# A decoder layer on one core: one-hot operations on pairs of 16-bit values, gate steps spread equally, and some weight products in 512-column matmuls

## The chip, the core and the metric

The kernel runs on one core of a Trainium2 chip. The metric is the device time of one launch in microseconds, lower is better. The engines are TensorE (PE in the profile; PEld is its loading of weights), VectorE (DVE), ScalarE (ACT), GpSimd (POOL) and SyncE (SP), which issues most of the loads. They run side by side, each through its own list of instructions in order, and wait for each other by semaphores.

## The reference, cut to what matters

256 tokens and 16 meta tokens of width 2048 pass through one layer in fp32:

```
h    = layer_norm(concat(meta, x))
proj = h @ w_in          # pool 1024 | z 3072 | x 3072 | B 1024 | C 1024 | dt 48
mix  = concat(pool_mix(pool), ssd(x, B, C, dt) * silu(z), normed by group) @ w_out
h    = layer_norm(ALPHA * h + mix)
q    = h @ wq            # 8 heads x 2 x 128: scores against 128 keys each,
                         # top 16 of each side, top 16 of the 256 sums -> i1, i2, gate
act  = gelu(h . u[i1 * 128 + i2])                       # 8 x 16 of 16384 experts a token
out  = layer_norm(ALPHA * h + sum_k gate_k * act_k * v[i1 * 128 + i2])
```

## The kernel before

Every product with a weight is made from two parts. A value is split into a high part (float32r, a rounded copy) and a low part (the rest), and three of the four products are summed in PSUM: high weight x high input, high weight x low input, low weight x high input. Weights come in units of 128 x 1024 (eight blocks of 128 x 128) in the order of `W_ORDER`; `next_unit` (line 116) issues the load on SP's queue three units ahead, ScalarE copies the high part `wh` (line 129), VectorE subtracts for the low part `wl` (line 130), with three buffers of each. `mm_unit` (line 199) makes the 24 matmuls of a unit, eight for each of the three products, 256 to 272 columns each: `wh` with the high input, `wh` with the low input, `wl` with the high input. A block of 128 output columns takes two units (`kh` 0 and 1).

The stages follow each other: layer norm and transposition; the `w_in` stage (72 blocks; in each of eight groups two for B and C, three for x, three for z, with the SSD work of the group before as `side` steps between units, by `tick`); the `w_out` stage, whose matmuls have 512 columns of the weight as the moving operand; the second layer norm, into `h1H` and `h1L`; 16 blocks of `wq` with the routing as side steps; 128 blocks of `u` (`u_block`, line 612); and the `v` stage.

The kernel doesn't gather rows of `u`. It computes `h . u` for all 16384 experts, densely, with the experts on partitions, and multiplies by a dense gate. `gate_steps` (line 750) makes the gate for four tokens at a time, in 64 steps for each half of the experts (half 1 while blocks 0 to 63 of u run, half 0 while blocks 64 to 127 run). The routing leaves the indices `iT` and the gates `gT` (a high and a low part) transposed, with the 128 chosen slots of a token on partitions. A step makes three one-hot tiles in fp16: `o2` (VectorE, 4 x 128: iota equal to the second index), `oe` (VectorE, 4 x 64: iota equal to the first index), and `o1` (GpSimd, 4 x 2 x 64: `oe` times the two gate parts). Eight matmuls of 64 columns per step multiply `o2` by `o1`. Each of these tiles has two buffers, and the matmuls of a step are issued with the one-hots of the step after it. Every two steps the PSUM tile `pg` is full: for half 1 ScalarE writes it into the tile `a1` as the gate that u's activations will be multiplied with (line 622); for half 0 VectorE multiplies it into `a0`, which already holds the activations (line 784).

In blocks 0 to 63 the number of gate steps after block b is

```python
n = -(-left // max(62 - b, 1))
tick(n)
left -= n
```

from the block on in which the routing is through (`left` starts at 65: 64 steps and one that only issues the last matmuls). In blocks 64 to 127 it is one and two in turn.

When a half is complete, `flag_steps` and `slot_steps` find for each expert row whether a token of either half of the tokens chose it, and give it a slot (`pos`). `scatter` (line 723) writes the activation rows of one block to `acd` in DRAM, by an indirect DMA on POOL's queue: for half 1 as blocks 72 to 122 pass, straight from `pos`; for half 0 from the last u blocks on, from small copies (`paced`) that VectorE makes behind the product of a block. The `v` stage begins with two dense blocks (`a_dense`), then SP loads slots of rows (`ac`, line 998), POOL gathers the rows of `v` that belong to them (`rawv`, line 1003), and TensorE multiplies; `a_split` (line 1015) splits the activations into `v_scr`. `ac` lies in the memory of `a1`; `v_scr` and the residual `rr` lie in that of `h1L` and `h1H`.

The order of instructions on each engine is not that of the source alone: a scheduler of the framework orders them at build time by its own estimates of cost, except where `keep_in_program_order` or `issue_after` pins them. Dependences and buffer releases are tracked tile by tile.

Of the kernel before, what the change touches and what calls it, by code (L numbers as in the profile page):

```python
# [2 lines left out]

# [1 line left out]

# [18 lines left out]
NL1 = 3  # L24
NQ1 = 3
NLB = 4
NDB = 2


# [33 lines left out]
def tile_layer(ctx: ExitStack, tc: tile.TileContext, x, meta, pk, pk48, w_in, w_dt, w_pool,  # L63
# [129 lines left out]

    front = ExitStack()
    hTp = front.enter_context(tc.tile_pool(name="hTp", bufs=1))
    hTH = hTp.tile([P, KC, L], F32R, name="hTH")
    hTL = hTp.tile([P, KC, L], F32R, name="hTL")

    def mm_unit(ps, xh, xl, kh, m, n, t0=0):

# [270 lines left out]
    for g in range(NG):  # L471
        bT = conv(24 + g, 0, "bT", 2)
        cc = conv(32 + g, 12, "cc", 2)
        xT = [conv(3 * g + j, 0, "xT", 6) for j in range(3)]
        zs = []
        side.append(group_steps(g, bT, cc, xT, zs))
        for j in range(3):
            pz = proj(NMETA)
            z = sp.tile([P, T], F32, tag="zs", name="zs", bufs=4)
            act.activation(z, pz[:, :T], AF.Silu)  # L480
            zs.append(z)


# [65 lines left out]

    lws = ExitStack()  # L550
    h1ps = []

    def w_out_body1(i):
        if i == 0:
            h1ps.append(ctx.enter_context(tc.tile_pool(name="h1p", bufs=1, side="right", reuse_waits="tile")))
            h1ps.append(h1ps[0].tile([P, KC, T], F32R, tag="h1H", name="h1H"))
            h1ps.append(h1ps[0].tile([P, KC, T], F32R, tag="h1L", name="h1L"))
            lw = lws.enter_context(tc.tile_pool(name="lw", bufs=1, side="right", reuse_waits="tile"))
            hold(range(2 + 144 + 64 - NL1, 2 + 144 + 64), lw)

# [10 lines left out]
                dve.bn_stats(sts[tt][:, c], hs[tt][:, cs])  # L571
    lp = lnp[0]
    lws.close()
    h1p, h1H, h1L = h1ps
# [37 lines left out]
    def u_block(b):  # L612
        ps = ps_tile("psu")
        for kh in range(2):
            mm_unit(ps, h1H, h1L, kh, P, T)
        if b < 64:
            act.activation(a_half[0][:, b, :T], ps[:, :T], AF.Gelu)
        else:

            act.activation(ps[:, :T], ps[:, :T], AF.Gelu)  # L620
            g = a_half[1][:, b - 64, :T]
            i = dve.tensor_mul(g if b < P - NDB else a_dense[:, b - (P - NDB)], g, ps[:, :T])  # L622
            if pos[0] is not None and n_sc[0] < HALF[0][1]:

                tc.keep_in_program_order(i)
# [94 lines left out]
    paced = []  # L720
    behind = [None]

    def scatter(half, b):
        at = paced.pop() if paced and not half else pos[half][:, b:b + 1]
        with tc.issue_after(behind[0].ins):
            i = pool.indirect_dma_start(  # L726
                out=acd[half][:, :], out_offset=bass.IndirectOffsetOnAxis(ap=at, axis=0),
                in_=a_half[half][:, b, :], in_offset=None)

        i = getattr(i, "ins", i)  # L730
        if b:
            tc.declare_no_dep(i, group=f"rows{half}", reason="rows of their own")
        tc.add_to_no_dep_group(f"rows{half}", i)

    def scatter_0():
        if n_sc[0] < HALF[0][1]:
            scatter(0, n_sc[0])
            n_sc[0] += 1

    def zero_steps():  # L740
# [9 lines left out]
    def gate_steps(half):  # L750


        io = iota[:, half * 64:(half + 1) * 64]
        pg = None
        ohs = []
        t0 = 0
        while t0 < T or ohs:
            wait = half == 0 and ranked[1] is not None
            if t0 < T and not wait:
                o2 = ohp.tile([P, 4, P], F16, tag="o2", name="o2", bufs=2)  # L760
                oe = ohp.tile([P, 4, 64], F16, tag="oe", name="oe", bufs=2)
                o1 = ohp.tile([P, 4, 2, 64], F16, tag="o1", name="o1", bufs=2)
                i1, i2 = (it[:, t0:t0 + 4].unsqueeze(2) for it in iT)
# [94 lines left out]
    def softmax_steps():  # L858
        for tt in range(2):
# [12 lines left out]
                pe.transpose(ps[:, i * P:(i + 1) * P], s[:, tt], ident)  # L872
            ts = slice(tt * P, (tt + 1) * P)
            for i in range(2):
                dve.tensor_copy(iT[i][:, ts], ps[:, i * P:(i + 1) * P])
            gs = rp.tile([P, P], F32, tag="gs", name="gs")
            dve.tensor_scalar(gs, ps[:, 2 * P:3 * P], GSC, None, ALU.mult)
            dve.tensor_copy(gT[:, ts, 0], gs)
            dve.tensor_sub(gT[:, ts, 1], gs, gT[:, ts, 0])
            yield  # L880

    for j in range(16):
        if j < NQ1:
            ps = pre[j]
            tick()
        else:
            ps = ps_tile("psq1")
            mm_unit(ps, h1H, h1L, 0, P, T)
            tick()
        mm_unit(ps, h1H, h1L, 1, P, T)  # L890
        tick()
        act.copy(qT[:, j, :], ps[:, :T])
# [10 lines left out]
    a_dense = slp.tile([P, NDB, T], F32, name="a_dense")  # L903
# [4 lines left out]
    iT = [ohp.tile([P, T], F16, name=f"iT{i}", bufs=1) for i in range(2)]  # L908
    gT = ohp.tile([P, T, 2], F16, name="gT", bufs=1)
    def flag_tick(n):  # L910
        while n and flagq:
            if next(flagq[0], flagq) is flagq:
# [5 lines left out]
    for b in range(64):  # L918
        u_block(b)
        if a_half[1] is None:  # L920
            tick(RT_TICKS)
            if not side:
# [22 lines left out]

    for b in range(64, 128):
        u_block(b)
        if pos[1] is not None:
            due = min(b - 64, -(-(P - NDB - 64) * (b - 72) // 50), P - NDB - 64)
            while n_sc[1] < due:  # L950
                scatter(1, n_sc[1])
                n_sc[1] += 1
        if side:
            tick(2 if b % 2 else 1)
            flag_tick(1)
        else:
            if paced:
                scatter_0()
            rank_0()
    drain()  # L960
    while pos[0] is None:
        rank_0()
    while n_sc[1] < P - NDB - 64:
        scatter(1, n_sc[1])
        n_sc[1] += 1


    rrt = h1p.tile([P, 2, D], F32, tag="h1H", name="rr")
    rr = [rrt[:, tt] for tt in range(2)]
    v_scr = h1p.tile([P, 16, T], F32R, tag="h1L", name="v_scr")  # L970
    ap1s.close()
# [43 lines left out]
    def a_split(i):  # L1015
# [9 lines left out]
        src = a_dense[:, b - (P - NDB)] if what == "d" else acs[i]  # L1025
# [155 lines left out]
```

## Time and profile before

| | |
|---|---|
| median of 3 runs | 2069.78 us (2066.89 to 2072.77) |
| profiled execution | 2070.15 us, its span 2068.5 us |
| mean granted TensorE clock | 0.993 |
| PE busy | 2012.2 us (97%), 14780 matmuls |
| DVE busy | 1573.7 us (76%) |
| ACT busy | 1115.4 us (54%) |
| POOL busy | 519.6 us (25%) |
| stages in the span (from the timeline) | w_in to about 510 us, w_out to 690, wq to 797, u to 1584, v to the end |

The profile is one execution. A busy time is the union of an engine's instructions; matmuls overlap in it, so a matmul's own duration is not its price, and the distance between the starts of two is. Numbers at the end of tile names are left out, so `o1` and `o2` are both `o` in the rows (o2 is written at line 764, o1 at 768). A wait in brackets is the idle time of the engine before an instruction, with what ended it.

### The profile page before, as it was taken

The page shows a single profiled execution, that of the slowest core. Times are in us where ns is not written, and L with a number is a line of the kernel's source. Part 1 is how long each engine was busy: PE and PEld are TensorE (multiplying, and loading weights), DVE is VectorE, ACT ScalarE, POOL GpSimd, SP SyncE. Part 2 cuts the span into 40 slices and gives each one's busy share as a digit, 9 for nine tenths or more (in the row PEclk, how much of TensorE's full clock was granted, in tenths as well). Part 3 has the DMA queues.
Part 4 walks back from the last instruction along what each step waited for, and adds up shares of the span by engine and source line. Part 5 has one row for each costly group of instructions (what it writes and reads, how often), then busy time and mean ns, then how long its engine had stood idle before and what let it go on. Part 6 is the DMA issues. An engine that isn't in the chain of part 4 may idle for free. (4 is left out here: it accounts for less than half of the span.)

```text
span 2068.5 us, 37549 instructions
## 1 busy us (share of the span) xinstructions
PE 2012.2 (97%) x14780; PEld 1859.8 (90%) x14780; DVE 1573.7 (76%) x2542; ACT 1115.4 (54%) x1637; POOL 519.6 (25%) x423
## 2 busy tenths in 40 slices
PE   7999999999999899999899999999999999999997
PEld 6999999999878799999899999999998777878885
DVE  6767777777654878999899979999954555656667
ACT  6457777777433544445459573333343555555563
POOL 1000000000000000000455525566334674232231
PEclk9999999999999999999999999999999999999999
DMA  5555555554775465665445556666678999778884
GB/s 160 187 179 173 177 180 177 174 178 160 255 235 197 158 204 175 184 183 175 150 146 167 173 173 196 199 191 197 199 223 270 300 323 330 273 268 288 295 310 150
DMA packets 113970, 430.75 MB, mean 208 GB/s; under 512 B 14112, under 2 KB 27808, under 8 KB 98800
## 3 DMA queue, kind: packets, MB, share of 16 engines
q1 hardware_dynamic: 89168, 282.29, 44.5%
q0 software_dynamic: 24336, 145.53, 19.7%
q8 instruction: 116, 1.90, 0.4%
q10 hardware_dynamic: 288, 0.52, 0.1%
q14 instruction: 62, 0.51, 0.1%
HBM read 407.20 MB, written 21.09 MB: 207 GB/s over the span
## 5 line engine op out<-in xcount | busy, mean ns | idle before, releaser
L129 ACT CAST wh<-raw 128x1024 fp32r<-128x1024 f32 (+1 forms) x502 | 525.8, 1047 | 662.3 <-PE psu L204 352.2
L130 DVE TENSOR_TENSOR wl<-raw,wh 128x1024 fp32r<-128x1024 f32 (+1 forms) x502 | 629.9, 1256 | 277.8 <-ACT wh L129 264.0
L130 DVE TENSOR_TENSOR wl<-rawv,wh 128x1024 fp32r<-128x1024 f32 x210 | 256.8, 1224 | 171.0 <-ACT wh L129 160.1
L1040 PE MATMUL psv<-wh,v_scr 128*128 128x512 f32 x1304 | 363.2, 398 | 11.4 <-ACT v_scr L1027 6.3
L129 ACT CAST wh<-rawv 128x1024 fp32r<-128x1024 f32 x210 | 220.3, 1049 | 205.8 <-PE psv L1040 109.0
L768 POOL TENSOR_TENSOR o<-oe,gT 128x512 f16<-128x512 f16 x128 | 200.1, 1574 | 475.7 <-DVE oe L766 291.7
L1040 PEld LDWEIGHTS psv<-wh,v_scr 128*128 128x128 f32 x1304 | 245.8, 190 | 75.4 <-ACT v_scr L1027 8.8
L204 PE MATMUL psu<-h1H,wh 128*128 128x256 f32 x2048 | 292.6, 285 | 0.0
L204 PE MATMUL psu<-h1L,wh 128*128 128x256 f32 x2048 | 286.2, 282 | 0.0
L204 PE MATMUL psu<-h1H,wl 128*128 128x256 f32 x2048 | 284.3, 281 | 0.0
L204 PEld LDWEIGHTS psu<-h1H,wh 128*128 128x128 f32 x2048 | 261.5, 189 | 0.0
L204 PEld LDWEIGHTS psu<-h1L,wh 128*128 128x128 f32 x2048 | 261.2, 189 | 0.0
L204 PEld LDWEIGHTS psu<-h1H,wl 128*128 128x128 f32 x2048 | 260.9, 188 | 0.0
L1040 PE MATMUL psv<-wl,v_scr 128*128 128x512 f32 x652 | 206.2, 395 | 0.0
L1003 POOL DMA_INDIRECT rawv<-in_v,ac x105 | 123.6, 1177 | 236.2 <-DVE wl L130 195.8
L204 PE MATMUL psj<-hTH,wh 128*128 128x272 f32 (+5 forms) x1168 | 177.3, 294 | 1.3 <-ACT hTH L185 0.8
L204 PE MATMUL psj<-hTL,wh 128*128 128x272 f32 (+5 forms) x1168 | 166.1, 284 | 0.0
L204 PE MATMUL psj<-hTH,wl 128*128 128x272 f32 (+5 forms) x1168 | 165.9, 284 | 0.0
L726 POOL DMA_INDIRECT acd<-a,flags x114 | 136.6, 1199 | 94.1 <-DVE a L622 32.6
L204 PEld LDWEIGHTS psj<-hTH,wh 128*128 128x128 f32 (+1 forms) x1168 | 154.2, 189 | 5.0 <-ACT hTH L185 1.8
L204 PEld LDWEIGHTS psj<-hTL,wh 128*128 128x128 f32 (+1 forms) x1168 | 151.9, 187 | 0.2
L204 PEld LDWEIGHTS psj<-hTH,wl 128*128 128x128 f32 (+1 forms) x1168 | 151.6, 187 | 0.0
(252 smaller groups left out, 2234.1 us busy)
## 6 DMA issues: line engine op xcount, KB each, us to landing
raw<-in_u SPq DMA_DIRECT2D x256, 512.0 KB
raw<-in_w_in SPq DMA_DIRECT2D x144, 512.0 KB
raw<-in_w_out SPq DMA_DIRECT2D x64, 512.0 KB
raw<-in_wq SPq DMA_DIRECT2D x32, 512.0 KB
ac<-acd SPq DMA_DIRECT2D x105, 128.5 KB
clb<-cd POOLq DMA_DIRECT2D x8, 816.0 KB
x<-in_x SPq DMA_DIRECT2D x4, 512.0 KB
gb<-in_ln_nat POOLq DMA_DIRECT2D x2, 1024.0 KB
```

Of the source, the lines that this page charges most:

```text
L129: act.copy(wh[:, :n], raw[:, :n])
L130: dve.tensor_sub(wl[:, :n], raw[:, :n], wh[:, :n].bitcast(F32))
L204: pe.matmul(ps[:m, :n], w[:, k * m:(k + 1) * m], xx[:, kh * 8 + k, t0:], start=first and k == 0, stop=last and k == 7)
L726: i = pool.indirect_dma_start(out=acd[half][:, :], out_offset=bass.IndirectOffsetOnAxis(ap=at, axis=0), in_=a_half[half][:, b, :], in_offs ...
L768: behind[0] = pool.tensor_mul(o1, oe.unsqueeze(2).to_broadcast([P, 4, 2, 64]), gT[:, t0:t0 + 4, :].unsqueeze(3).to_broadcast([P, 4, 2, 64]))
L1003: i = pool.indirect_dma_start(out=raw, out_offset=None, in_=v[:, :], in_offset=bass.IndirectOffsetOnAxis(ap=ac.bitcast(U32)[:, T:T + 1], a ...
L1040: pe.matmul(po[tt][n], mm[:, tt * P:(tt + 1) * P], w[:, c:c + 512], start=first, stop=end)
```

## The change

- `mm_both` is new: the high and the low input lie in one tile (`hT`, `h1`), and `wh` multiplies both in one matmul of 512 columns; `wl` multiplies the high part in one of 256. A unit has 16 matmuls in place of 24. The two halves of the PSUM bank are then added: ScalarE copies one, VectorE adds the other. It is used for the 24 blocks of z, for blocks 3 to 15 of wq, and for blocks 108 to 127 of u. The other blocks keep `mm_unit`.
- The one-hots: `iT` and `gT` hold every value twice, side by side, and the operands are read as pairs, so that the innermost dimension has two elements with a step of one. `o1` is made by two multiplications on VectorE; GpSimd has none left.
- Gate steps of half 1 are given out in equal shares over the blocks that are left.
- Scatter positions of half 1 are copied behind a block's product too, up to two in one copy, and scatters of both halves follow these copies (`due`, `paced_scatters`).
- `a_dense` and the first block's split activations move to buffers of the one-hot pool; `rr` and `v_scr` get a pool of their own in the memory of `h1`, which is freed as a whole.

```diff
+U_BOTH = 108
...
-    hTH = hTp.tile([P, KC, L], F32R, name="hTH")
-    hTL = hTp.tile([P, KC, L], F32R, name="hTL")
+    hT = hTp.tile([P, 2, KC, L], F32R, name="hT")
+    hTH, hTL = hT[:, 0], hT[:, 1]
+
+    def mm_both(ps, xx, kh, t0=0):
+        wh, wl = next_unit()
+
+        def low():
+            for k in range(8):
+                pe.matmul(ps[:, :T], wl[:, k * P:(k + 1) * P], xx[:, 0, kh * 8 + k, t0:], start=False, stop=False)
+
+        if kh:
+            low()
+        for k in range(8):
+            pe.matmul(ps, wh[:, k * P:(k + 1) * P], xx[:, :, kh * 8 + k, t0:],
+                      start=kh == 0 and k == 0, stop=kh == 1 and k == 7)
+        if not kh:
+            low()
...
         for j in range(3):
-            pz = proj(NMETA)
+            pz = ps_tile("psz")
+            for kh in range(2):
+                mm_both(pz, hT, kh, NMETA)
+                tick()
             z = sp.tile([P, T], F32, tag="zs", name="zs", bufs=4)
-            act.activation(z, pz[:, :T], AF.Silu)
+            act.copy(z, pz[:, T:])
+            dve.tensor_add(z, z, pz[:, :T])
+            act.activation(z, z, AF.Silu)
...
-                mm_unit(ps, h1H, h1L, kh, P, T)
+            if b < U_BOTH:
+                mm_unit(ps, h1H, h1L, kh, P, T)
+            else:
+                mm_both(ps, h1, kh)
+        if b >= U_BOTH:
+            part = ohp.tile([P, T], F32, tag="o2", name="part", bufs=2)
+            act.copy(part, ps[:, T:])
+            dve.tensor_add(ps[:, :T], part, ps[:, :T])
...
-                paced.append(slp.tile([P, 1], U32, tag="paced", name="paced", bufs=3))
-                tc.keep_in_program_order(dve.tensor_copy(paced[0], pos[0][:, n_sc[0]:n_sc[0] + 1]))
+            for half, n in due(b):
+                if first:
+                    tc.keep_in_program_order(i)
+                    first = False
+                at = slp.tile([P, 2], U32, tag="paced", name="paced", bufs=4)
+                k = n_sc[half] + sum(m for h, m, _ in paced if h == half)
+                tc.keep_in_program_order(dve.tensor_copy(at[:, :n], pos[half][:, k:k + n]))
+                paced.append((half, n, at))
+
+    def due(b):
+        if pos[1] is not None and n_sc[1] < P - NDB - 64:
+            n = min(b - 63, -(-(P - NDB - 64) * (b - 71) // 50), P - NDB - 64) - n_sc[1]
+            while n > 0:
+                yield 1, min(n, 2)
+                n -= 2
+        if pos[0] is not None and n_sc[0] < HALF[0][1]:
+            yield 0, 1
...
+                def pairs(ap):
+                    return ap.rearrange("p t (i e) -> p t i e", e=2)
+
+                def wide(ap, n):
+                    return ap.unsqueeze(2).to_broadcast([P, 4, n, 2])
+
-                dve.tensor_tensor(o2, iota[:, None, :].to_broadcast([P, 4, P]), i2.to_broadcast([P, 4, P]),
+                dve.tensor_tensor(pairs(o2), pairs(iota[:, None, :].to_broadcast([P, 4, P])), wide(i2, 64),
                                   ALU.is_equal)
-                dve.tensor_tensor(oe, io[:, None, :].to_broadcast([P, 4, 64]), i1.to_broadcast([P, 4, 64]),
+                dve.tensor_tensor(pairs(oe), pairs(io[:, None, :].to_broadcast([P, 4, 64])), wide(i1, 32),
                                   ALU.is_equal)
-                behind[0] = pool.tensor_mul(o1, oe.unsqueeze(2).to_broadcast([P, 4, 2, 64]),
-                                            gT[:, t0:t0 + 4, :].unsqueeze(3).to_broadcast([P, 4, 2, 64]))
+                for q in range(2):
+                    dve.tensor_mul(pairs(o1[:, :, q]), pairs(oe), wide(gT[:, t0:t0 + 4, q], 32))
...
-            mm_unit(ps, h1H, h1L, 0, P, T)
+            mm_both(ps, h1, 0)
...
+            mm_both(ps, h1, 1)
+            tick()
+            act.copy(qT[:, j, :], ps[:, T:])
+            dve.tensor_add(qT[:, j, :], qT[:, j, :], ps[:, :T])
...
+                first = b
         else:
-            n = -(-left // max(62 - b, 1))
+            n = 0
+            while left * (62 - first) > GATE_STEPS * max(61 - b, 0):
+                n += 1
+                left -= 1
             tick(n)
-            left -= n
...
+        if i == 0:
+
+            ah, al = (ohp.tile([P, T], F32R, tag="o2", name="a_first", bufs=2) for _ in range(2))
```

## Rows read from the trace of the kernel before

**Rows 1.** Busy us by engine (x instructions), then TensorE's granted clock, DMA share, GB/s.
```profile
1000.00:1050.00 50.00, 40.01 (x417) 38.78 (x415) 42.03 (x47) 22.05 (x26) 25.78 (x18) 0.97 0.42 127
1050.00:1100.00 50.00, 50.00 (x518) 49.68 (x519) 47.23 (x49) 34.08 (x69) 26.62 (x18) 1.00 0.52 159
```

**Rows 2.** Timeline of ScalarE: start us, us, what; Gelu of successive u blocks.
```profile
991.31 0.38 ACT L617 ACTIVATE a<-psu 128x256 f32<-128x256 f32 x1
997.00 0.38 ACT L617 ACTIVATE a<-psu 128x256 f32<-128x256 f32 x1
...
1003.27 0.37 ACT L617 ACTIVATE a<-psu 128x256 f32<-128x256 f32 x1
...
1054.79 0.38 ACT L617 ACTIVATE a<-psu 128x256 f32<-128x256 f32 x1
```

**Rows 3.** Timeline of all engines, around the third step of a block.
```profile
1021.27 3.58 DVE L764 TENSOR_TENSOR o<-iota,iT 128x512 f16<-128x512 f16 x3
1022.85 0.61 PE L779 MATMUL pg<-o,o 128*128 128x64 f16 x8 [2.42 <-DVE o L764]
1023.27 2.06 PE L204 MATMUL psu<-h1H,wh 128*128 128x256 f32 x8
```

**Rows 4.** Who waited for whom, whole span: us, times, longest us.
```profile
PE pg L779 <- DVE o L764: 10.2, 7, 2.4
```

**Rows 5.** Groups by line and shape, whole span: busy us, mean ns, idle before.
```profile
L768 POOL TENSOR_TENSOR o<-oe,gT 128x512 f16<-128x512 f16 x128 | 200.1, 1574 | 475.7 <-DVE oe L766 291.7 <-PE pg L779 173.2 <-DVE cs L714 5.6
L764 DVE TENSOR_TENSOR o<-iota,iT 128x512 f16<-128x512 f16 x128 | 147.5, 1178 | 0.0
L622 DVE TENSOR_TENSOR a<-a,psu 128x256 f32<-128x256 f32 x62 | 25.5, 412 | 0.0
L1028 DVE TENSOR_TENSOR v_scr<-ac,v_scr 128x128 fp32r<-128x128 f32 x51 | 14.5, 284 | 0.2 <-ACT v_scr L1027 0.2
```

**Rows 6.** Timeline in half 0: an o2 alone, and a wait for GpSimd.
```profile
1353.90 0.68 DVE L764 TENSOR_TENSOR o<-iota,iT 128x512 f16<-128x512 f16 x1
...
1357.34 0.39 PE L779 MATMUL pg<-o,o 128*128 128x64 f16 x8 [1.06 <-POOL o L768]
```

**Rows 7.** Timeline in the w_in stage, a z block.
```profile
221.24 1.23 DVE L130 TENSOR_TENSOR wl<-raw,wh 128x1024 fp32r<-128x1024 f32 x1
...
225.87 1.10 PE L204 MATMUL psj<-hTH,wh 128*128 128x256 f32 x8
...
227.74 1.10 PE L204 MATMUL psj<-hTH,wl 128*128 128x256 f32 x8
```

**Rows 8.** Timeline of TensorE in the u stage, 256 columns.
```profile
856.79 1.11 PE L204 MATMUL psu<-h1L,wh 128*128 128x256 f32 x8
...
869.13 1.12 PE L204 MATMUL psu<-h1H,wl 128*128 128x256 f32 x8
```

**Rows 9.** Timeline of TensorE in the w_out stage, 512 columns.
```profile
519.85 1.07 PE L497 MATMUL pso<-wh,mixH 128*128 128x512 f32 x4
...
521.66 1.07 PE L497 MATMUL pso<-wl,mixH 128*128 128x512 f32 x4
```

**Rows 10.** Timeline of TensorE in the v stage, 512 columns.
```profile
1700.70 1.10 PE L1040 MATMUL psv<-wh,v_scr 128*128 128x512 f32 x4
...
1710.46 1.10 PE L1040 MATMUL psv<-wh,v_scr 128*128 128x512 f32 x4
```

**Rows 11.** Timeline at the start of the v stage.
```profile
1585.01 0.41 DVE L622 TENSOR_TENSOR a_dense<-a,psu 128x256 f32<-128x256 f32 x1
...
1599.30 3.63 PE L1040 MATMUL psv<-wh,v_scr 128*128 128x512 f32 x8 [3.65 <-ACT v_scr L1027]
```

**Rows 12.** Busy us by engine while half 0's gate is made.
```profile
1200.00:1490.00 290.00, 288.61 (x2783) 286.44 (x2782) 272.18 (x338) 124.95 (x218) 155.10 (x113) 1.00 0.63 193
```

**Rows 13.** Groups of VectorE by line and shape, 1200 to 1490 us.
```profile
L764 DVE TENSOR_TENSOR o<-iota,iT 128x512 f16<-128x512 f16 x62 | 57.8, 944 | 0.0
...
L766 DVE TENSOR_TENSOR oe<-iota,iT 128x256 f16<-128x256 f16 x60 | 31.5, 531 | 1.6 <-PE psl L689 1.6
```

More of the change, by code (lines that the diff above doesn't have):

```diff
@@ L1 @@
 import math
-from contextlib import ExitStack
+from contextlib import ExitStack, nullcontext
 import numpy as np
@@ L551, in tile_layer @@
     h1ps = []
+    h1s = ExitStack()
     def w_out_body1(i):
         if i == 0:
-            h1ps.append(ctx.enter_context(tc.tile_pool(name="h1p", bufs=1, side="right", reuse_waits="tile")))
-            h1ps.append(h1ps[0].tile([P, KC, T], F32R, tag="h1H", name="h1H"))
-            h1ps.append(h1ps[0].tile([P, KC, T], F32R, tag="h1L", name="h1L"))
+            h1ps.append(h1s.enter_context(tc.tile_pool(name="h1p", bufs=1, side="right", reuse_waits="tile")))
+            h1ps.append(h1ps[0].tile([P, 2, KC, T], F32R, name="h1"))
             lw = lws.enter_context(tc.tile_pool(name="lw", bufs=1, side="right", reuse_waits="tile"))
@@ L573, in tile_layer @@
     lws.close()
-    h1p, h1H, h1L = h1ps
+    _, h1 = h1ps
+    h1H, h1L = h1[:, 0], h1[:, 1]
     mv = lp.tile([P, 2, 2], F32, name="mv1")
@@ L621, in u_block, with paced_scatters @@
             g = a_half[1][:, b - 64, :T]
-            i = dve.tensor_mul(g if b < P - NDB else a_dense[:, b - (P - NDB)], g, ps[:, :T])
-            if pos[0] is not None and n_sc[0] < HALF[0][1]:
-                tc.keep_in_program_order(i)
-                paced.append(slp.tile([P, 1], U32, tag="paced", name="paced", bufs=3))
-                tc.keep_in_program_order(dve.tensor_copy(paced[0], pos[0][:, n_sc[0]:n_sc[0] + 1]))
+            if b >= P - NDB:
+                a_dense.append(ohp.tile([P, T], F32, tag="o1", name="a_dense", bufs=2))
+            i = dve.tensor_mul(g if b < P - NDB else a_dense[-1], g, ps[:, :T])
+            first = True
+            for half, n in due(b):
[14 more added lines that the diff above has]
+            yield 0, 1
+    def paced_scatters():
+        while paced:
+            half, n, at = paced.pop(0)
+            for k in range(n):
+                scatter(half, n_sc[half], at[:, k:k + 1])
+                n_sc[half] += 1
     acd = {h: dram.tile([sum(rows_of(h)[2:]) * P, ROW], F32, name=f"acd{h}") for h in HALF}
@@ L721, in tile_layer, with scatter @@
     behind = [None]
-    def scatter(half, b):
-        at = paced.pop() if paced and not half else pos[half][:, b:b + 1]
-        with tc.issue_after(behind[0].ins):
+    def scatter(half, b, at):
+        with tc.issue_after(behind[0].ins) if behind[0] is not None else nullcontext():
             i = pool.indirect_dma_start(
@@ L736, in scatter_0 @@
         if n_sc[0] < HALF[0][1]:
-            scatter(0, n_sc[0])
+            scatter(0, n_sc[0], pos[0][:, n_sc[0]:n_sc[0] + 1])
             n_sc[0] += 1
@@ L874, in softmax_steps @@
             for i in range(2):
-                dve.tensor_copy(iT[i][:, ts], ps[:, i * P:(i + 1) * P])
+                dve.tensor_copy(iT[i][:, ts], ps[:, i * P:(i + 1) * P].unsqueeze(2).to_broadcast([P, P, 2]))
             gs = rp.tile([P, P], F32, tag="gs", name="gs")
             dve.tensor_scalar(gs, ps[:, 2 * P:3 * P], GSC, None, ALU.mult)
-            dve.tensor_copy(gT[:, ts, 0], gs)
-            dve.tensor_sub(gT[:, ts, 1], gs, gT[:, ts, 0])
+            gs2 = gs.unsqueeze(2).to_broadcast([P, P, 2])
+            dve.tensor_copy(gT[:, ts, 0], gs2)
+            dve.tensor_sub(gT[:, ts, 1], gs2, gT[:, ts, 0])
             yield
@@ L887, in tile_layer @@
             ps = ps_tile("psq1")
-            mm_unit(ps, h1H, h1L, 0, P, T)
+            mm_both(ps, h1, 0)
             tick()
-        mm_unit(ps, h1H, h1L, 1, P, T)
-        tick()
-        act.copy(qT[:, j, :], ps[:, :T])
+        if j < NQ1:
+            mm_unit(ps, h1H, h1L, 1, P, T)
+            tick()
+            act.copy(qT[:, j, :], ps[:, :T])
+        else:
+            mm_both(ps, h1, 1)
+            tick()
+            act.copy(qT[:, j, :], ps[:, T:])
+            dve.tensor_add(qT[:, j, :], qT[:, j, :], ps[:, :T])
         if j == 0:
@@ L902, in tile_layer @@
     slp = ctx.enter_context(tc.tile_pool(name="slots", bufs=1))
-    a_dense = slp.tile([P, NDB, T], F32, name="a_dense")
+    a_dense = []
     ap0s = ExitStack()
@@ L907, in tile_layer @@
     number(0)
-    iT = [ohp.tile([P, T], F16, name=f"iT{i}", bufs=1) for i in range(2)]
-    gT = ohp.tile([P, T, 2], F16, name="gT", bufs=1)
+    iT = [ohp.tile([P, T, 2], F16, name=f"iT{i}", bufs=1) for i in range(2)]
+    gT = ohp.tile([P, T, 2, 2], F16, name="gT", bufs=1)
     def flag_tick(n):
@@ L947, in tile_layer @@
         u_block(b)
[L948 to L952, printed above, removed]
+        paced_scatters()
         if side:
@@ L956, in tile_layer @@
         else:
-            if paced:
-                scatter_0()
             rank_0()
@@ L962, in tile_layer @@
         rank_0()
[L963 to L968, printed above, removed]
+    assert n_sc[1] == P - NDB - 64
+    ap1s.close()
+    h1s.close()
+    vrp = ctx.enter_context(tc.tile_pool(name="vrp", bufs=1, side="right", reuse_waits="tile"))
+    rrt = vrp.tile([P, 2, D], F32, name="rr")
     rr = [rrt[:, tt] for tt in range(2)]
-    v_scr = h1p.tile([P, 16, T], F32R, tag="h1L", name="v_scr")
-    ap1s.close()
+    v_scr = vrp.tile([P, 16, T], F32R, name="v_scr")
     vp = ctx.enter_context(tc.tile_pool(name="vp", bufs=1, side="right", reuse_waits="tile"))
@@ L1023, in a_split @@
         ah, al = v_scr[:, s], v_scr[:, s + 1]
+        if i == 0:
+            ah, al = (ohp.tile([P, T], F32R, tag="o2", name="a_first", bufs=2) for _ in range(2))
         c = slice(tts[0] * P, (tts[-1] + 1) * P)
-        src = a_dense[:, b - (P - NDB)] if what == "d" else acs[i]
+        src = a_dense[b - (P - NDB)] if what == "d" else acs[i]
         tc.keep_in_program_order(act.copy(ah[:, c], src[:, c]))
```

2 lines of the change are left out of this document (1 added, 1 removed).

## The prediction

> **What bounds the kernel now.** I read the windows first, then the pace of the blocks, the waits of TensorE, the prices of the one-hot operations, and last the spacing of matmuls. TensorE is the bound nearly everywhere: between 1050 and 1100 us, as in most windows, it is busy without a break, while VectorE is busy for 47 of 50 us; in the 50 us before, it is busy for only 40, at a mean granted clock of 0.97 [rows 1]. That hole is the gate stage of half 1. ScalarE applies Gelu once per block of u, so the starts of that instruction give the block's period: 5.69 us for a block without gate matmuls, 6.27 us with two gate steps (0.29 us a step), but 51.52 us for the next six blocks, which have three steps each [rows 2]. Six such blocks would need 6 x (6.27 + 0.29) = 39.4 us; 12.2 us are lost. The reason stands in the timeline: VectorE makes three o2 tiles in 3.58 us, about 1.5 us apart, and TensorE waits 2.42 us for the first of them, which starts 0.84 us into the wait; afterwards eight matmuls of 256 columns take 2.06 us instead of about 0.95, which is the lower of the two clock levels [rows 3]. Over the run, gate matmuls wait 10.2 us for o2 [rows 4]. The rest of the hole is this slow clock.
>
> Why the third step of a block is late: the o2, oe and o1 tiles have two buffers, so the first two steps of a block can be made ahead, and the third only when the first step's matmuls have read theirs. What a step's VectorE and GpSimd work costs is then on the path.
>
> **The change, part by part, against this run's own 2070.15 us** (0.4 us over the median of the runs shown).
>
> *Equal steps.* The old rule gives ceil(left / (62 - b)) steps: seven blocks of three, then two each. With 65 steps the six long blocks behind two short ones fit only a start at block 32 (the very first step issues no matmuls); from there the new rule gives five in block 33, two in most, and three in four blocks. Of the five, the first issues no matmuls and the next two are made ahead, so two are late; with the four others there are again six late steps. Only their spacing and price change.
>
> *One-hots.* Before, a step costs VectorE 1178 ns for o2, plus oe, and GpSimd 1574 ns for o1 (128 of each, 200 us of GpSimd) [rows 5]. The mean of o2 is not its own price: alone it takes 0.68 us [rows 6], and over twice that where GpSimd's multiplications run beside it [rows 3]. The change removes all 128 GpSimd multiplications, so that loss goes, and adds two VectorE multiplications of 256 elements per step. No row has 16-bit operands of which all lie in adjacent pairs, so I bound the price. At two elements a cycle, o2 should cost what 256 elements cost now, 0.41 us, and oe and both halves of o1 what 128 elements cost, 0.28 us each [rows 5]: 1.26 us per step. At one element a cycle it is 0.68 us [rows 6] and three times 0.41 us: 1.91 us. I take 1.26: the old operands repeat single elements, and exactly that is what the doubling ends.
>
> [...]
>
> A late step now stops TensorE for 1.26 us and an assumed 0.1 us of hand-over, less the 0.29 us of the matmuls of the step before it: 1.07 us, or 6.4 us for six if TensorE stands still each time. If matmuls of u are put ahead of every second one, those are covered: 3.2 us. The gain then lies between 12.2 - 6.4 = 5.8 us and 12.2 - 3.2 = 9.0 us; I take the middle, **7.4 us**. The bounds are wider: 12.2 us if no step is late, and 12.2 - 6 x (1.07 + 0.84) = 0.7 us if VectorE is 0.84 us late for each, as before [rows 3]. In half 0 there are one or two steps per block, none late in this way; one wait of 1.06 us for GpSimd's product goes [rows 6]: **1.1 us**.
>
> *VectorE's load.* In half 0 it is busy for 272 of 290 us, while TensorE works almost throughout [rows 12], and o2 and oe cost 944 + 531 ns a step [rows 13]. At 1.26 us a step VectorE becomes lighter. This frees no time by itself, as TensorE is the bound there. The copies of scatter positions that are now made for half 1 as well, at most one of about 0.15 us per block, fit into what is freed. The doubling of iT and gT adds eight instructions' worth of 128 more elements, about 1 us, under TensorE's work.
>
> *Matmuls of 512 columns.* Two products with the same wh become one: 8 pairs a unit, 24 blocks of z, 13 of wq and 20 of u with two units each, so 384 + 208 + 320 = 912 pairs. Matmuls of 256 columns follow each other every 116.9 ns in z (16 in 1.87 us) [rows 7] and every 118.65 ns in u (104 in 12.34 us) [rows 8]; a pair takes 233.8 or 237.3 ns. Those of 512 columns follow every 226.3 ns in the w_out stage (8 in 1.81 us) [rows 9] and every 232.4 ns in the v stage (42 in 9.76 us) [rows 10]. For z, next to the w_out stage, I take 226.3: 384 x 7.5 ns = 2.9 us. For the other 528, between 4.9 and 11.0 ns, the middle: 4.2 us. Together **7.1 us**; the bounds are 8.7 us with 226.3 throughout and 3.1 us with 232.4, and zero, since no row reads its 512 columns from two places.
>
> [...]
>
> The halves must be added: per block one ScalarE copy from PSUM (0.38 us, like the Gelu of the same shape [rows 2]) and one VectorE addition (0.41 us [rows 5]); wq had the copy already. What hides them is the lead of the weights: in z a wl is finished at 222.47 and its unit starts at 225.87, 3.4 us later [rows 7]. In the second unit of a block, wl is now needed at once and no longer behind the wh products; the lead still covers that. Without cover each block would lose up to 0.8 us, 46 us over 57 blocks.
>
> *Start of the v stage.* Behind the last block, VectorE's product at 1585.01 frees a1, SP then loads the scattered rows, they are gathered, and TensorE, through with the two dense blocks, waits until 1599.30 (3.65 us) [rows 11]. The copy and addition stand ahead of that product, so the chain ends 0.8 us later, with hand-overs **1 us** (0 to 2). The first dense block's own buffers let TensorE begin earlier, but it then waits longer for the same gather: nothing.
>
> **Sum:** 2070.15 - 7.4 - 1.1 - 7.1 + 1.0 = 2055.55, so 2055.5 us. The bounds give 2070.15 - 12.2 - 1.1 - 8.7 = 2048 and 2070.15 - 0.7 - 3.1 + 2 = 2068.
>
> **Rivals.**
> 1. *The long matmul saves nothing*, because the jump between the high and the low part costs what the second matmul did. Against it: w_out and v run faster at 512 [rows 9, 10]; for it: those read one run. 2055.5 + 7.1 = 2062.6.
> 2. *The pairs are not taken*, and a step costs 1.91 us. Late steps cost 6 x 1.72 = 10.3 us or half, so the gain there is about 4.5. In half 0, 62 steps x (1.91 - 1.475) = 27 us are added to a VectorE that has 18 us left [rows 12, 13]: 9 us. 2070.15 - 4.5 - 1.1 - 7.1 + 1 + 9 = about 2067, no change that can be told.
> 3. *ScalarE stands still in z: slower.* Its Silu waits for the addition, which queues on VectorE behind decay and convolution work; ScalarE's next weight cast waits behind Silu, and VectorE's wl behind that cast. For it: both queues run in order, and the order is fixed by a scheduler, not by the source. Against it: 3.4 us of lead [rows 7]. A delay of d costs 24 x (d - 3.4) us: at 4.0 the gain is gone, from 4.3 the kernel is slower, at 4.6 it takes 2055.5 + 28.8 = 2084.
> 4. *Everything at its best*, with no late step and a better order at the start of v: 2043 to 2048.
>
> **How the numbers follow.** Chances: the forecast 0.64 (its own range 2048 to 2068), no gain from long matmuls 0.10, no pairs 0.10, slower 0.08, best 0.08. A change under 0.3% (6.2 us) can't be told from none here: faster is below 2064, slower above 2076. The forecast, save a tenth of it, the first rival, save a third, and the best case are faster: 0.73. The second rival and those remainders are the same: 0.17. Slower gets 0.10, the third rival and a little for a bad order elsewhere. The range 2043 to 2070 leaves out the third rival and the outer ends of the others.
>
> **What would show it.** o2 at about 0.41 us and oe and o1 at about 0.28 us; at 0.68 and 0.41 us the second rival is right. Blocks 33 to 40 with a period near 6.3 us and at most one much longer; gate waits of TensorE down from 11 us to below 6. Long matmuls every 226 to 232 ns in z and u; 237 would be the first rival. TensorE without idle time at psz, and wl still ahead there; gaps in z would be the third. At the start of v a wait longer than 3.65 us. The prediction is wrong if the gap in the gate stage stays, or if a wait appears in a stage that now has none.

## The result, and the profile after

The changed kernel takes 2056.88 us (median of 4 runs, 2052.72 to 2058.43); the kernel before, beside it, 2069.88 us. The ratio is 0.9934, 95% interval 0.9913 to 0.9955: 13.0 us faster, between 9 and 18. The profiled execution took 2058.43 us, with a span of 2056.7 us and a mean granted clock of 0.994 of full speed.

The windows of the kernel after (busy us of TensorE, weight loads, VectorE, ScalarE and GpSimd, then TensorE's granted clock, DMA share and GB/s) answer to [rows 1, 12]:

```profile
1000.00:1050.00 50.00, 48.49 (x505) 48.10 (x504) 33.98 (x79) 26.76 (x31) 0.00 (x0) 1.00 0.49 159
1050.00:1100.00 50.00, 50.00 (x517) 49.52 (x516) 34.95 (x82) 36.22 (x85) 0.00 (x0) 1.00 0.52 161
1200.00:1490.00 290.00, 289.89 (x2703) 283.76 (x2700) 245.07 (x511) 123.80 (x207) 62.53 (x52) 1.00 0.62 195
```

The hole of ten microseconds between 1000 and 1050 us has shrunk to 1.5 us, at full clock, and VectorE is lighter in both gate stages although it has taken over GpSimd's multiplications. Why it is lighter stands in the groups by line of VectorE (o1 at L829, o2 at L824, oe at L826; busy us, mean ns, idle before), which answer to [rows 5, 13]:

```profile
L829 DVE TENSOR_TENSOR o<-oe,gT 128x256 f16<-128x256 f16 x256 | 62.3, 284 | 0.0
L824 DVE TENSOR_TENSOR o<-iota,iT 128x512 f16<-128x512 f16 x128 | 53.4, 417 | 1.5 <-PE pg L839 1.4
L826 DVE TENSOR_TENSOR oe<-iota,iT 128x256 f16<-128x256 f16 x128 | 32.5, 285 | 2.3 <-PE psl L744 1.6
```

o2 costs 417 ns, oe 285 and each half of o1 284: 1.27 us a step. ScalarE's Gelu per block of u, now at L648, gives the pace of the gate stage as in [rows 2] (start us, us, what):

```profile
987.97 0.38 ACT L648 ACTIVATE a<-psu 128x256 f32<-128x256 f32 x1
993.67 0.38 ACT L648 ACTIVATE a<-psu 128x256 f32<-128x256 f32 x1
1002.34 0.38 ACT L648 ACTIVATE a<-psu 128x256 f32<-128x256 f32 x1
1008.60 0.38 ACT L648 ACTIVATE a<-psu 128x256 f32<-128x256 f32 x1
...
1027.36 0.38 ACT L648 ACTIVATE a<-psu 128x256 f32<-128x256 f32 x1
1035.60 0.38 ACT L648 ACTIVATE a<-psu 128x256 f32<-128x256 f32 x1
...
1054.36 0.38 ACT L648 ACTIVATE a<-psu 128x256 f32<-128x256 f32 x1
```

The period is 6.25 us, with a long block of 8.67 us and later one of 8.24. TensorE's waits (us in total, times, longest) have changed places, compared with [rows 4]:

```profile
PE pg L839 <- DVE o L829: 4.5, 3, 1.5
PE psv L1109 <- ACT v_scr L1096: 6.0, 3, 4.5
PE psv L1109 <- ACT a_first L1096: 1.7, 1, 1.7
```

Gate matmuls wait three times 1.5 us, now for o1. What a wait consists of shows in VectorE's instructions at the one of 1027.79 to 1029.30 us:

```profile
1027.48 1.23 DVE L131 TENSOR_TENSOR wl<-raw,wh 128x1024 fp32r<-128x1024 f32 x1 [1.61 <-ACT wh L130]
...
1028.63 0.42 DVE L824 TENSOR_TENSOR o<-iota,iT 128x512 f16<-128x512 f16 x1
1028.96 0.49 DVE L829 TENSOR_TENSOR o<-oe,gT 128x256 f16<-128x256 f16 x2
...
1029.30 0.19 PE L839 MATMUL pg<-o,o 128*128 128x64 f16 x1 [1.50 <-DVE o L829]
```

VectorE is busy with a low part `wl` of the weights, so o2 starts 0.84 us into the wait; o2 and the first half of o1 follow, and oe had been made before. The two other waits are built in the same way. The 1.7 us and the longest of the 6.0 us (4.5) are the start of v. Its timeline answers to [rows 11]:

```profile
1571.37 1.04 ACT L130 CAST wh<-raw 128x1024 fp32r<-128x1024 f32 x1 [2.41 <-PE psu L212]
...
1572.32 0.36 ACT L645 COPY part<-psu 128x256 f32<-128x256 f32 x1
1572.44 1.23 DVE L131 TENSOR_TENSOR wl<-raw,wh 128x1024 fp32r<-128x1024 f32 x1 [2.10 <-ACT wh L130]
...
1573.59 0.42 DVE L646 TENSOR_TENSOR psu<-part,psu 128x256 f32<-128x256 f32 x1
1574.04 0.37 ACT L651 ACTIVATE psu<-psu 128x256 f32<-128x256 f32 x1 [1.05 <-DVE psu L646]
...
1574.45 0.41 DVE L655 TENSOR_TENSOR a_dense<-a,psu 128x256 f32<-128x256 f32 x1
...
1588.89 1.58 PE L1109 MATMUL psv<-wh,v_scr 128*128 128x512 f32 x3 [4.50 <-ACT v_scr L1096]
```

The copy of the half sum (`part`) stands behind a weight cast of 1.04 us on ScalarE, and the addition behind the wl of 1.23 us on VectorE. The long matmuls last, as TensorE's timeline shows them in z and in the last blocks of u:

```profile
236.74 3.88 PE L212 MATMUL psz<-hT,wh 128*128 128x512 f32 x16
240.46 2.05 PE L207 MATMUL psz<-hT,wl 128*128 128x256 f32 x16
242.35 2.03 PE L212 MATMUL psz<-hT,wh 128*128 128x512 f32 x8
...
1539.30 2.06 PE L207 MATMUL psu<-h,wl 128*128 128x256 f32 x16
1541.20 3.88 PE L212 MATMUL psu<-h,wh 128*128 128x512 f32 x16
1544.92 1.34 PE L207 MATMUL psu<-h,wl 128*128 128x256 f32 x10
```

Sixteen long ones take 3.72 us in both places, 232.5 ns each: the spacing of the v stage [rows 10], not that of w_out [rows 9]. A block is 5.62 us long (1539.30 to 1544.92), not 5.69.

**Where the time came from.** The starts of the same instructions in the two traces (Gelus, first matmuls of a stage) give a ledger. Gates of half 1 (Gelu of block 31 to that of block 63): 214.61 to 208.21 us, -6.4. Half 0 (blocks 64 to 107): -1.5. For the long matmuls one trace against one is too rough, since a stage varies by 1 us or so between executions; with the experiments below there are eleven traces that have them in z and wq and three that have not:

| stage | plain, mean of 3 | with long matmuls, mean of 11 | difference |
|---|---|---|---|
| z (first w_in matmul to first w_out matmul) | 491.75 | 489.97 (standard deviation, sd, 0.80) | -1.8 |
| wq (its first matmul to the first of u) | 96.89 | 96.06 (sd 0.39) | -0.8 |
| u, Gelu of block 107 to last u matmul | 114.95 | 113.62 (9 traces, sd 0.03) | -1.3 |

Together -3.9 us. At the start of v, the last matmul of u to the end of the wait for the first gathered weights went from 15.9 us (1583.42 to 1599.30 in the trace before) to 18.0 us (1570.93 to 1588.89): +2.1. (Nine traces with merged last blocks have 17.5 to 18.8 us there, the three without merging 15.5 to 15.9.) The terms sum to -9.7 us. The spans differ by 11.7 us; the rest lies in stages that the change does not touch (v behind its first gather is 1.3 us shorter), and is of the size of their scatter. No run took back the new scatter copies or the moved buffers alone, so what these are worth is not shown.

### The profile page after: what moved, and what is told of

Same layout as the page of the kernel before. It is cut to its first block, busy times and chain, and to the rows that moved or that the text cites. A ratio compares the mean times of both kernels' runs of the same rounds, so it can differ in the third digit from the quotient of the medians.

```text
span 2056.7 us, 35911 instructions
## 1 busy us (share of the span) xinstructions
PE 2006.8 (98%) x13868; PEld 1813.1 (88%) x13868; DVE 1508.7 (73%) x2909; ACT 1120.5 (54%) x1674; POOL 319.1 (16%) x295
## 5 line engine op out<-in xcount | busy, mean ns | idle before, releaser
L222 PE MATMUL psu<-h,wh 128*128 128x256 f32 x3456 | 454.6, 284 | 0.0
L222 PEld LDWEIGHTS psu<-h,wh 128*128 128x128 f32 x3456 | 425.5, 188 | 0.5
L222 PE MATMUL psu<-h,wl 128*128 128x256 f32 x1728 | 240.0, 281 | 0.0
L222 PE MATMUL psj<-hT,wh 128*128 128x272 f32 (+4 forms) x1568 | 219.5, 292 | 1.3 <-ACT hT L186 0.8
L222 PEld LDWEIGHTS psu<-h,wl 128*128 128x128 f32 x1728 | 220.3, 188 | 0.0
L222 PEld LDWEIGHTS psj<-hT,wh 128*128 128x128 f32 (+1 forms) x1568 | 203.1, 188 | 4.7 <-ACT hT L186 1.8
L1109 PEld LDWEIGHTS psv<-wl,v_scr 128*128 128x128 f32 x644 | 121.7, 189 | 28.6
L222 PE MATMUL psj<-hT,wl 128*128 128x272 f32 (+4 forms) x784 | 112.9, 286 | 0.0
L222 PEld LDWEIGHTS psj<-hT,wl 128*128 128x128 f32 (+1 forms) x784 | 103.0, 186 | 0.0
L212 PE MATMUL psz<-hT,wh 128*128 128x512 f32 x384 | 96.2, 396 | 0.0
```

What stands on the lines that cost most here:

```text
L212: pe.matmul(ps, wh[:, k * P:(k + 1) * P], xx[:, :, kh * 8 + k, t0:], start=kh == 0 and k == 0, stop=kh == 1 and k == 7)
L222: pe.matmul(ps[:m, :n], w[:, k * m:(k + 1) * m], xx[:, kh * 8 + k, t0:], start=first and k == 0, stop=last and k == 7)
L1109: pe.matmul(po[tt][n], mm[:, tt * P:(tt + 1) * P], w[:, c:c + 512], start=first, stop=end)
```

## The experiments

Each was timed beside the kernel before on the same chip. The changed kernel itself, timed again so, gave 2058.43 us and 0.9940 (0.9921 to 0.9960). Theory: TensorE was held up in the gate stage by the price of a step, and the pairs and GpSimd's absence lower it; the long matmuls save some nanoseconds a pair. Rivals: only the even spread counts; only the pairs, or only GpSimd, count; the long matmuls save nothing.

**Products of 256 columns again** in z, wq and u:

```
-            for kh in range(2):
-                mm_both(pz, hT, kh, NMETA)
+            pz = proj(NMETA)
...
-U_BOTH = 108
+U_BOTH = P
```

> The changed kernel with every product in matmuls of 256 (to 272) columns again and no adding of halves; all else as changed. The forecast's term of 7.1 us for the long matmuls and 1 us for the later start of the v stage says 2056.9 + 7.1 - 1 = 2063 us, with the u stage 20 x 0.17 = 3 us longer and the z blocks 3 us. What the changed kernel's own trace says instead (long matmuls 231 to 232 ns apart, so about 4 us in all, and a start of the v stage that lost 2 us): 2056.9 + 4 - 2 = 2059 us, the v stage's wait back to about 3.7 us.

Measured: 2062.17 us, 0.9967 (0.9955 to 0.9979). Gate waits are unchanged (4.5 us, three times), but half 1 took 209.73 us, 1.5 more than in the changed kernel, at a granted clock of 0.98 between 1000 and 1050 us, in a stage that the edit does not touch. The long matmuls are worth about 0.3% by the ratios, 5.6 or 6.8 us against the two timings of the changed kernel, with an interval of some 5 us either way. By the traces it is less, 3.9 us from the table minus some 2 us that the additions cost at the start of v, which this interval just allows. They save something, so the first rival (they save nothing, 2062.6 us for the changed kernel) did not come; its figure is near the time of this kernel, which has none.

**The old rule for the steps**, one-hots as changed:

```
-            n = 0
-            while left * (62 - first) > GATE_STEPS * max(61 - b, 0):
-                n += 1
-                left -= 1
+            n = -(-left // max(62 - b, 1))
             tick(n)
+            left -= n
```

> The changed kernel with the old rule for the number of gate steps per block (seven blocks of three, then two each). If the price of a late step is what counts, there are six late steps either way and the time stays within 1.5 us of 2057. If the even spread was what removed the waits, the waits of TensorE for gate tiles grow from 4.5 us to about 9 and the time to 2061 to 2063.

Measured: 2059.14 us, 0.9948 (0.9935 to 0.9961), and gate waits of 4.5 us in three again. The even spread is worth nothing that can be told.

**Single elements, all on VectorE:**

```
-                dve.tensor_tensor(pairs(o2), pairs(iota[:, None, :].to_broadcast([P, 4, P])), wide(i2, 64),
-                                  ALU.is_equal)
+                dve.tensor_tensor(o2, iota[:, None, :].to_broadcast([P, 4, P]), i2.to_broadcast([P, 4, P]),
+                                  ALU.is_equal)
```

and likewise oe and o1.

> The changed kernel with all one-hot work on VectorE, but each index and gate read as a single element again. o2 takes 0.68 us and oe and the two o1 products 0.41 us each, 1.91 us a step. If pairs carry the gain, late steps cost 0.65 us more each (six: 4 us) and VectorE in half 0 has 27 us of work more than the trace of before, 9 us beyond what is free there: 2061 to 2070 us. If taking GpSimd's products away carries it, at most 2 us are lost: below 2059 us.

Measured: 2069.07 us, 0.9999 (0.9986 to 1.0012): by the median the whole gain is gone. Its groups by line, its window of half 0's gates, TensorE's waits for one-hots over the run, and the longest of these in the timeline:

```profile
L829 DVE TENSOR_TENSOR o<-oe,gT 128x256 f16<-128x256 f16 x256 | 97.4, 418 | 0.0
L824 DVE TENSOR_TENSOR o<-iota,iT 128x512 f16<-128x512 f16 x128 | 87.5, 684 | 0.6 <-PE pg L839 0.6
```
```profile
1200.00:1490.00 290.00, 284.59 (x2647) 278.95 (x2646) 275.38 (x501) 119.07 (x199) 71.24 (x51) 0.99 0.58 189
```
```profile
PE pg L839 <- DVE o L829: 11.1, 6, 4.5
```
```profile
1376.66 0.23 PE L839 MATMUL pg<-o,o 128*128 128x64 f16 x1 [4.46 <-DVE o L829]
...
1377.48 3.55 PE L222 MATMUL psu<-h,wh 128*128 128x256 f32 x15
...
1382.43 2.06 PE L222 MATMUL psu<-h,wh 128*128 128x256 f32 x16
```

The traced loss lies mostly in the other half of the gates than in [rows 1]. Half 1 takes 209.84 us here, only 1.6 us over the changed kernel; half 0 takes 270.47 instead of 262.09 (Gelu of block 64 to that of block 107). Of these 8.4 us, 7.2 fall in one block: VectorE has no free microsecond between 1340 and 1380 us, TensorE waits 4.5 us for o1, and then runs at a lower granted clock (15 matmuls take 3.55 us, 16 a little later 2.06; the granted clock is 0.89 between 1360 and 1380 us and 0.94 in the 20 us behind). The traced execution is the shortest of twelve, 2062.89 us; what the median has above it, some 6 us, no trace shows.

**Pairs for o2 and oe, o1 on GpSimd:**

```
-                for q in range(2):
-                    dve.tensor_mul(pairs(o1[:, :, q]), pairs(oe), wide(gT[:, t0:t0 + 4, q], 32))
+                pool.tensor_mul(o1, oe.unsqueeze(2).to_broadcast([P, 4, 2, 64]),
+                                gT[:, t0:t0 + 4, :, 0].unsqueeze(3).to_broadcast([P, 4, 2, 64]))
```

> The changed kernel with o2 and oe on pairs, but o1 made by GpSimd in one product as before. If GpSimd's products slow VectorE, o2 goes from 0.42 us to 0.8 us or more where they overlap and the weights' low parts grow from 1.22 us again; a late step then takes o2, oe and a GpSimd product of 1.05 us or more: waits for gate tiles above 8 us, 2060 to 2066 us. If only the price of the pairs counts, o2 stays at 0.42 us, VectorE is lighter by 0.57 us a step, and the time stays within 2 us of 2057.

Measured: 2066.53 us, 0.9983 (0.9974 to 0.9992). Its groups by line, TensorE's waits for one-hots, and a gate step in its timeline:

```profile
L824 DVE TENSOR_TENSOR o<-iota,iT 128x512 f16<-128x512 f16 x128 | 107.3, 862 | 1.7 <-PE pg L839 1.7
...
L828 POOL TENSOR_TENSOR o<-oe,gT 128x512 f16<-128x512 f16 x128 | 202.0, 1592 | 473.3 <-DVE oe L826 285.6 <-PE pg L839 183.7 <-DVE cs L769 3.9
```
```profile
PE pg L839 <- DVE o L824: 8.9, 6, 2.2
```
```profile
1028.12 3.15 POOL L828 TENSOR_TENSOR o<-oe,gT 128x512 f16<-128x512 f16 x2 [3.10 <-PE pg L839]
1029.10 2.45 DVE L824 TENSOR_TENSOR o<-iota,iT 128x512 f16<-128x512 f16 x2
...
1030.42 0.41 PE L839 MATMUL pg<-o,o 128*128 128x64 f16 x8 [2.15 <-DVE o L824]
```

The mirror image in the trace, which is again of the shortest execution (2061.41 us): half 0 is as good as changed (261.60 us), half 1 almost as bad as before (213.68). The paired o2 takes 862 ns on average; the two of the row, for instance, are over at 1031.55, 0.28 us after the two multiplications of GpSimd (1031.27). So the two parts of the one-hot change need each other: taking GpSimd away mends half 1, and only with pairs can VectorE carry the extra work in half 0.

**Half of a block's gate steps between its two units**, in the changed kernel and in the kernel before (the rest behind the block as now; in the changed kernel at most four steps a block):

```
         for kh in range(2):
+            if kh:
+                tick(mid)
...
-        u_block(b)
+        u_block(b, n // 2)
...
-            tick(n)
+            tick(n - n // 2)
```

> The changed kernel with half of a block's gate steps of half 1 issued between its two units (and at most four in a block), so that no block has more than two steps in a row. If late steps are late because the one-hot tiles have two buffers, the 4.5 us of gate waits go (to below 1.5) and the time falls to 2052 to 2054. If VectorE's order is the cause, the waits stay at 3 to 5 us.

> The kernel before, with its GpSimd multiply and single elements kept, and half of a block's gate steps of half 1 put between its two units. Theory (two buffers of one-hots make the third step of a burst late, and it is the burst that costs): bursts of two steps fit the two buffers, most of the 10.2 us of waiting goes, 2061 to 2065 us. Rival (the pace of the one-hot operations themselves is too slow for the steps however they are spread): the waits stay above 7 us, 2068 to 2070 us.

In the changed kernel, TensorE's waits for one-hots all but vanish in the stage (990 to 1190 us):

```profile
PE pg L841 <- DVE o L831: 0.3, 1, 0.3
```

and half 1 takes 205.38 us, 2.8 less; but the time is 2057.37 us, 0.9934 (0.9913 to 0.9954), not to be told from the changed kernel, and not the 2052 to 2054 expected. In the kernel before the same edit gave 2068.34 us, 0.9984 (0.9972 to 0.9995). The forecast of 2061 to 2065 failed; the time is the rival's, though the waits are not (5.6 us over the run, where it had above 7). The waits of its stage (990 to 1200 us) and a window say why:

```profile
PE pg L781 <- DVE o L766: 4.8, 12, 0.8
```
```profile
1020.00:1050.00 30.00, 27.44 (x283) 26.08 (x283) 30.00 (x33) 15.53 (x19) 15.57 (x13) 1.00 0.45 140
```

The long waits are split into twelve short ones and the granted clock stays at 1.00, but VectorE, beside GpSimd, has no free microsecond in 30. Half 1 takes 214.61 us in the trace before, 211.45 with the steps split, 208.21 with the cheaper steps of the change, and 205.38 with both. The two buffers, then, make the third step late, and the price of a step is the larger part of what that costs.

**The 512 columns in one run of memory** (h1 laid out so that the high and low parts are neighbours):

```
-            h1ps.append(h1ps[0].tile([P, 2, KC, T], F32R, name="h1"))
+            h1ps.append(h1ps[0].tile([P, KC, 2, T], F32R, name="h1"))
```

> The changed kernel with the high and the low part of h1 side by side for each block of 128 features, so that a long matmul of wq and u reads its 512 columns in one run. If the jump between two places costs the 5 ns that separate 231 from 226, long matmuls of wq and u follow every 226 to 227 ns and 528 of them save 2.5 us: about 2054.5. If the spacing comes from the stage (its DMA traffic), it stays at 231 and the time at 2057.

Measured: 2058.21 us, 0.9939 (0.9922 to 0.9955). Its long matmuls in u:

```profile
1538.85 3.90 PE L212 MATMUL psu<-h,wh 128*128 128x512 f32 x16
1542.58 2.06 PE L207 MATMUL psu<-h,wl 128*128 128x256 f32 x16
```

3.73 us for 16, 233 ns; before the edit it was 3.72 us. The jump between the parts costs nothing that shows there, nor in the time (2058.21 against 2058.43 us); why w_out has 226 ns and u 232 stays open.

**The last two blocks of u in 256-column products:**

```
-            if b < U_BOTH:
+            if b < U_BOTH or b >= U_END:
...
+U_END = 126
```

> The changed kernel with the last two blocks of u in matmuls of 256 columns, so that no copy and addition stand ahead of the last product that frees a1. If these lengthened the chain to the first gather by 1 us, as forecast, the wait of TensorE for the first gathered block falls from 4.5 us to about 3.7 and the 1.7 us ahead of the first dense block go too; two blocks lose 0.15 us: 2055 to 2056. If the start of v hangs on the order of ScalarE's other work, both waits stay: 2057.

Measured: 2061.13 us, 0.9949 (0.9932 to 0.9967); no gain, though its trace has 4.7 us more in w_out, which the edit does not touch (183.7 us against 179.1). TensorE begins v 0.1 us after u, not 2.1, but waits longer for the gather:

```profile
1573.72 1.12 PE L223 MATMUL psu<-h,wl 128*128 128x256 f32 x8
...
1576.19 0.41 DVE L656 TENSOR_TENSOR a_dense<-a,psu 128x256 f32<-128x256 f32 x1
...
1591.32 1.22 PE L1110 MATMUL psv<-wh,v_scr 128*128 128x512 f32 x2 [5.41 <-ACT v_scr L1097]
```

From the last u matmul (1574.57) it is 16.7 us, 1.2 less than changed. The way to the end of the last product is down from 3.9 us (1570.93 to 1574.86) to 2.0, as before; the gather behind it takes 14.7 us instead of 14.0, and why stays open.

**More merged blocks.** In blocks 0 to 63 the place that the Gelu writes can hold the copied half:

```
-            if b < U_BOTH:
+            if 64 <= b < U_BOTH:
...
+            part = a_half[0][:, b, :T] if b < 64 else ohp.tile([P, T], F32, tag="o2", name="part", bufs=2)
```

alone, with the steps between the units, and with the last two blocks plain:

> The changed kernel with 64 more merged blocks of the u product (blocks 0 to 63; the upper half of the sum is copied into the place that the Gelu then writes): 1,024 more 512-column matmuls in place of 2,048 of 256 columns. Theory (a merged pair saves the difference of the spacings in the trace after, 2 x 118.6 - 231.5, about 5.7 ns): 1,024 x 5.7 ns = 5.8 us less than the changed kernel, some 2051 us, and the Gelu of block 63 moves by that much against first psu. Rival A (the price of the first forecast, about 11 ns a pair): 11 us less, 2046 us. Rival B (the copy on ScalarE and the add on VectorE, 64 times each, hold up the casts of the next weights or the gate steps): no gain, 2056 us or more, with new waits of PE for wh or wl.

> The changed kernel with both additions: 64 more merged blocks, and half of a block's gate steps of half 1 between its two units. Theory: the two gains add, 5.8 us for the merged pairs and 2 to 3 us for the three waits of 1.5 us that are left, 2048 to 2050 us. Rival: the waits that are taken away come back as waits for the copy and the add, and the time is that of the kernel with more merged blocks alone.

> The kernel with 64 more merged blocks, and its last two blocks of u (126 and 127) in 256-column products again. Theory: in the traces so far the start of v costs 17.7 us from the last matmul of u to the end of the wait for the first gather with merged last blocks and 16.5 us with plain ones, so 1.2 us come back and 0.1 us of merged pairs is given up: 2052 us, ratio 0.991, with the first matmul of v 0.1 us instead of 2.1 us after the last of u. If the gain of the 64 merged blocks is real, this second timing of them (the pair of edits is the same kernel but for 1 us) falls between 0.989 and 0.993 as well. Rival: the gain of those blocks was chance, the merged pairs save what their spacing in blocks 0 to 63 shows and no more (2 to 3 us), and the ratio comes back to 0.993 to 0.995.

Measured: 2053.37 us, 0.9914 (0.9896 to 0.9932); 2059.99 us, 0.9950 (0.9934 to 0.9965); 2055.08 us, 0.9939 (0.9927 to 0.9952). The first is the fastest seen, but its twin, the third, falls where the rival put it. By the traces both save 3.6 us from the first matmul of u to the Gelu of block 64, of which 1.5 us are gate waits (3.0 us now, in five); so some 2 us for 1,024 pairs, less than the 5.8 us that the spacing promised. A version that surely beats the changed kernel was not found. The second shows that gains need not add: with copy, addition and gate steps at the same places, a gate step comes late again:

```profile
1103.68 0.56 PE L841 MATMUL pg<-o,o 128*128 128x64 f16 x8 [2.44 <-DVE o L831]
```

## Why the prediction was right, and where its sizes were off

The time (2055.5 against 2056.88 us), the direction and the mechanism came out. That the times are only 1.4 us apart is in part luck. Two of the four terms were mis-sized, both towards too much gain: the terms as found sum to -9.7 us, not -14.6. That is inside the interval of the measured gain (9 to 18 us), near its lower end; whether the 2 to 3 us between the ledger and the measured gain are scatter or a saving that no term names, the runs don't settle.

*Price of a step.* Taken as 0.41 + 3 x 0.28 = 1.26 us, measured 1.27. No row showed beforehand that pairs would be cheaper: the choice of 1.26 over 1.91 was my estimate, and of elements a cycle no run says anything, only of times. The kernel without pairs shows these: the doubling of operands alone takes o2 from 684 to 417 ns and each half of o1 from 418 to 284. The second rival, pairs not taken, was priced at about 2067 with 9 us lost in half 0; the kernel without pairs took 2069 and lost 8.4 us there. The agreement is in part luck. Its working adds 27 us to VectorE's 272 us in half 0, but VectorE rose only to 275: the one-hots took 24 us more (113.6 instead of 89.3), and the low parts of the weights 18 us less with GpSimd's multiplications gone, as their groups between 1200 and 1490 us show, in the kernel before and in that without pairs:

```profile
L130 DVE TENSOR_TENSOR wl<-raw,wh 128x1024 fp32r<-128x1024 f32 x95 | 130.1, 1374 | 17.8 <-ACT wh L129 17.1
```
```profile
L131 DVE TENSOR_TENSOR wl<-raw,wh 128x1024 fp32r<-128x1024 f32 x92 | 112.0, 1219 | 12.2 <-ACT wh L130 12.1
```

What was lost is mostly one long wait and the lower granted clock behind it (4.5 us; 0.89 and then 0.94).

*Gates of half 1*: -7.4 forecast, -6.4 found, by two errors that nearly cancel. Only three late steps stop TensorE, as in the better of the two cases that were averaged, but each for 1.5 us, longer than the 1.07 us worked out. That sum has oe on the path, which is made ahead, and leaves out that VectorE comes 0.84 us late, behind a `wl`; the prediction has this only in its outer bound. So one sign missed: two of the blocks from 33 to 40 are much longer (8.67 and 8.24 us), not at most one. The slow clock of the hole (granted 0.50 while the eight matmuls of [rows 3] take 2.06 us) is gone in the changed kernel's trace, as assumed, with 1.00 between 1000 and 1050 us; in that of the kernel without long matmuls some of it is back (0.98). *Half 0*: -1.1 forecast, -1.5 found.

*Long matmuls*: -7.1 forecast, -3.9 found, or 4.3 ns for each of 912 pairs instead of 7.8. This is the step that failed in size: for z I took the spacing of the neighbouring w_out stage (226 ns), and for wq and u the middle between it and v's; u and z have the 232 ns of v.

*Start of v*: +1.0 forecast (0 to 2), +2.1 found. The two operations were priced at their own durations. Each also stood behind a weight operation of its engine, 1.04 us on ScalarE and 1.23 us on VectorE, and that was not counted: from the last u matmul to the end of the last product it is 3.9 us, before 2.0 (1583.42 to 1585.42). Without merging, the stretch to the end of the wait takes 15.5 us (last matmul of u at 1575.17, end of the wait at 1590.68).

*Cover elsewhere.* The copies and additions in z and wq cost nothing that shows; the third rival, ScalarE standing still in z, did not come.

## What to carry to other kernels

When two engines share a job and the wait is at their end, price the operations with the neighbour running and with it silent: here o2 took 0.68 us alone and 1.53 beside a multiplication of GpSimd, and, by the medians, the change without its pairs lost all of its 13 us, and without the move from GpSimd some 9 of them. For an operation put on a chain, count its own time and the instruction that its queue is busy with: at the start of v the copy of 0.36 us stood behind a cast of 1.04 us, and the addition of 0.42 us behind a wl of 1.23 us. And where a gain rests on a few nanoseconds times a thousand, take the smallest of the savings that the spacings in the trace allow.

## What the runs showed of the hardware that was not expected

By these traces, an o2 that started while a GpSimd multiplication ran did not run slowly, it seems, but stood still: with pairs on VectorE and o1 on GpSimd, the two o2s from 1029.10 us on ended 0.28 us after the end of the multiplication whether they had begun 0.24 or 0.98 us into it (lengths of 1.26 us against 0.42 alone); in the kernel before, with single elements, the first two of [rows 3] ended 0.55 us after it (1.53 against 0.68). A paired o2 that was already under way when GpSimd began (1031.68 us, GpSimd at 1031.90) took 0.41 us.
